# Hybrid decoder step on one core: where the first MLP's output is scaled for the time mixer, and when the residual is loaded

## The chip, the cores and the metric

The kernel runs on one core of a Trainium2 chip. Times are device microseconds of one execution, the median of three runs; the profile is of one further execution.

## The reference, cut to what matters

A decoder step of two layers: layer 0 mixes tokens with a Conformer convolution, layer 1 with RWKV-7 time mixing, and each is followed by a squared-ReLU MLP. The program has 1048 tokens (16 meta tokens, 1024 of the prompt, 8 decode tokens), a width of 1024 and a hidden width of 4096. What the change touches is the seam between the layers.

```python
def _rmsnorm(x, g):
    xf = x.astype(jnp.float32)
    y = xf * lax.rsqrt(jnp.mean(xf * xf, axis=-1, keepdims=True) + RMS_EPS)
    return (y * g.astype(jnp.float32)).astype(x.dtype)
...
def _rwkv7(h, shift_prev, S0, x_mix, ...):
    prev = jnp.concatenate([shift_prev[:, None, :].astype(h.dtype), h[:, :-1]], axis=1)
    xx = prev - h
    xr = h + xx * x_mix[0]      # and five more mixtures of h and xx
    ...
    out = ((yn + bonus).astype(h.dtype) * g) @ w_o
    return out, h[:, -1], S_final.astype(S0.dtype)
...
    for i in range(DEPTH):
        hn = _rmsnorm(h, norm_mix[i])
        ...                     # the mixer of this layer on hn
        h = h + out
        h = h + _sqrelu_mlp(_rmsnorm(h, norm_mlp[i]), w_mlp_in[i], w_mlp_out[i])
```

## The kernel before, in words

Activations lie with the width on the partitions: a tile of `[128, 8, n]` holds n tokens, the second index is the block of 128 channels (k-tile). The fp32 products are made of three fp32r matmuls of high and low parts: `split` (L159, L160) cuts a tile on ScalarE and VectorE or POOL, `load_w` (L165, L177, L182) loads and cuts weights, `mm3` (L211 to L213) multiplies.

The tokens are cut three ways. Layer 0 works on three groups G0 = (0, 352), (352, 348), (700, 348), as (first column, count). The RWKV mixer works on four groups G1 = (0, 272), (272, 256), (528, 256), (784, 264), called mixers 0 to 3 below. The mixer's output and the second MLP work on three groups G2 = (16, 328), (344, 352), (696, 352).

At the end of layer 0's MLP, `norm_out(g)` stores the residual h to `d_h` in DRAM, sums squares, makes the reciprocal root mean square `rs`, scales h in place by the norm's weights and `rs` (eight operations at L651, one for each k-tile) and stores the result to `d_hn`. `prepare(g)` of a mixer loads its columns of `d_hn` and the column before them into `hx` (L863, L865), makes the difference `xx` to the previous token (L869: six k-tiles on VectorE, two on POOL), and offers `mix(i, k)` (L892), which makes one k-tile of one of the six mixtures and splits it. `mixer_in(g)` makes the projections and the chunks' factors (names `rk`, `ab`, `wa`, `bv`), which go through DRAM; `advance` runs the recurrence over chunks of 64 tokens (`xa`, `sv`, `ni`), and its outputs go to `d_z`. `mixer_out(g)` loads the residual into h1 (L1633) and eight k-tiles of `d_z` into `zr` (L1639, three buffers), splits them, multiplies by `w_o` (tile `ps_oo`) and adds the products to h1 (L1643).

The stages overlap. The third group's first MLP with its `norm_out(2)` runs interleaved with mixer 0 (`beside_mixer`); what is left of it is finished before mixer 1 starts, where the pools of layer 0 are closed and those of the recurrence (`sv`, `xa`, set to zero on POOL) are opened in their place. `prepare(g+1)` runs inside the last phase of `mixer_in(g)`. `mixer_out(0)` runs while the recurrence goes on. Where instructions finally stand on each engine is decided when the program is built, by a scheduler that orders them by priorities and its own estimates; the tile framework inserts the waits.

Of the kernel before, what the change touches and what calls it, by code (L numbers as in the profile page):

```python
# [8 lines left out]
F32 = mybir.dt.float32  # L9
# [3 lines left out]
ALU = mybir.AluOpType  # L13
# [3 lines left out]
P = 128  # L17
D = 1024
KT = D // P
# [5 lines left out]
T = NP_TOK + DEC  # L25
# [5 lines left out]
G0 = [(0, 352), (352, 348), (700, 348)]  # L31
N0 = 352
G1 = [(0, 272), (272, 256), (528, 256), (784, 264)]
N1 = 272
# [14 lines left out]
def hybrid_step(tc, x_prompt, x_sample, state_conv, state_shift, state_wkv, meta_tokens,  # L49
# [8 lines left out]
    nc = tc.nc  # L58
    ctx = ExitStack()
    with ctx:  # L60
        def pool(stack, name, bufs, **kw):
            return stack.enter_context(tc.tile_pool(name=name, bufs=bufs, reuse_waits="tile", **kw))
# [10 lines left out]
        dram = pool(ctx, "dram", 1, space=bass.MemoryType.DRAM)  # L73
        d_x2 = dram.tile([P, KT, G0[2][1]], F32, name="d_x2")
        d_h = dram.tile([P, KT, T], F32, name="d_h")
        d_hn = dram.tile([P, KT, T], F32, name="d_hn")
        d_rk = dram.tile([P, KT, 2, T], F32, name="d_rk")
        d_ab = dram.tile([NCH, P, KT, 2, 2 * HS], F32, name="d_ab")
        d_v = dram.tile([NCH * HS, D], F32, name="d_v")
# [29 lines left out]
        for name, ap in vecs:  # L109
            n = ap.shape[0]  # L110
# [7 lines left out]
        def vec(name, i):  # L118
            c = col[name] + i
            return pvec[:, c:c + 1]  # L120

        cur = {}
# [34 lines left out]
        def split(hi, lo, src, eng_lo):  # L157

            nc.scalar.copy(hi, src)  # L159
            eng_lo.tensor_sub(lo, src, hi.bitcast(F32))  # L160
# [80 lines left out]
        def tt(name, tag):  # L241
            return cur["tmp"].tile([P, cur["n"]], F32, name=name, tag=tag)
# [19 lines left out]
        def mean_bcast(accs, n, name):  # L262

            ps = bank(f"st_{name}", "x")
            for i, acc in enumerate(accs):
                nc.tensor.matmul(ps[:, :n], ones_d, acc[:, :n], start=i == 0, stop=i == len(accs) - 1)
            return ps

        def square_sums(n, name, place, engs, tag="acc"):


            out, first = [], []

            def add(k, src):
                sq = place(k)
                nc.scalar.activation(sq, src, AF.Square)
                i = k % len(engs)
                if k >= KT - 2:
                    out.append(sq)
                elif k < len(engs):  # L280
                    first.append(sq)
                else:
                    if k < 2 * len(engs):
                        out.append(stat(f"acc_{name}{i}", f"{tag}{i}", 1))
                        a, b = out[i][:, :n], first[i]
                    else:
                        a = b = out[i][:, :n]
                    engs[i].tensor_add(a, b, sq)
            return add, out

        def rstd_of(ps, n, eps_i, name, tag="rs", bufs=2):
            sd = stat(f"sd_{name}", "sd", 1)
            nc.scalar.activation(sd[:, :n], ps[:, :n], AF.Sqrt, bias=eps_t[:, eps_i:eps_i + 1])
            rs = stat(f"rs_{name}", tag, bufs)
            nc.vector.reciprocal(rs[:, :n], sd[:, :n])
            return rs
# [117 lines left out]
        with ExitStack() as le:  # L414
# [221 lines left out]
            def norm_out(g):  # L636

                c0, n = G0[g]
                hv = h[g][:, :, :n]
                nc.sync.dma_start(d_h[:, :, c0:c0 + n], hv)  # L640
                if g < 2:
                    add, parts = square_sums(n, f"d{g}", lambda k: u[g][:, k, :n], (nc.gpsimd,), "accd")
                else:
                    add, parts = square_sums(n, f"d{g}", lambda k: tt(f"sqd{k}", "t1")[:, :n], (nc.gpsimd, nc.vector))
                for k in range(KT):
                    add(k, hv[:, k, :])
                    yield MW / KT
                rs = rstd_of(mean_bcast(parts, n, f"d{g}"), n, 0, f"d{g}", "rs" if g < 2 else "rsm")
                yield 1
                for k in range(KT):  # L650
                    nc.vector.scalar_tensor_tensor(hv[:, k, :], hv[:, k, :], vec("norm_mix", KT + k), rs[:, :n],  # L651
                                                   op0=ALU.mult, op1=ALU.mult)
                    yield 1
                nc.sync.dma_start(d_hn[:, :, c0:c0 + n], hv)
# [32 lines left out]
            with ExitStack() as s:  # L687
# [35 lines left out]
                for i, parts in enumerate((((1, rwkv_w1[0]), (4, rwkv_a1[0])), ((5, rwkv_g1[0]),))):  # L723
                    own, prev = (xin.tile([P, D], F32, name=f"lr{i}{s_}", tag="xt").rearrange("p (k c) -> p k c", k=KT) for s_ in "op")
                    w = P // len(parts)
# [128 lines left out]
        def prepare(g):  # L854

            c0, n = G1[g]
            npr = min(c0 + n, NP_TOK) - c0
            nm = lambda s, *a: f"{s}{g}" + "".join(f"_{x}" for x in a)

            hx = hnp.tile([P, KT, 1 + N1], F32, name=nm("hx"), tag="hx")  # L860
            if g == 0:
                nc.gpsimd.memset(hx[:, :, 0:1], 0.0)
                nc.sync.dma_start(hx[:, :, 1:1 + n], d_hn[:, :, :n])  # L863
            else:
                nc.sync.dma_start(hx[:, :, :1 + n], d_hn[:, :, c0 - 1:c0 + n])  # L865
            yield
            xx = hnp.tile([P, KT, N1], F32, name=nm("xx"), tag="xx")
            for k in range(KT):
                (nc.gpsimd if k % 3 == 2 else nc.vector).tensor_sub(xx[:, k, :npr], hx[:, k, 0:npr], hx[:, k, 1:1 + npr])  # L869
                yield  # L870
            if npr < n:
                sst = cur["raw"].tile([P, D], F32, name="sst", tag="raw")
                nc.scalar.dma_start(sst[:DEC, :], state_shift[0])
                pv = bank("pv", "x")
                for k in range(KT):
                    nc.tensor.transpose(pv[:, k * DEC:(k + 1) * DEC], sst[:DEC, k * P:(k + 1) * P], ident[:DEC, :DEC])
                sps = hnp.tile([P, KT, DEC], F32, name=nm("sps"), tag="sps")
                nc.scalar.copy(sps.rearrange("p k b -> p (k b)"), pv[:, :KT * DEC])
                nc.vector.tensor_sub(xx[:, :, npr:n], sps, hx[:, :, 1 + npr:1 + n])
                so = cur["raw"].tile([P, D], F32, name="so", tag="raw")  # L880
                for half in range(2):
                    pv = bank(f"pso{half}", "x")
                    for q in range(4):
                        nc.tensor.transpose(pv[:DEC + 1, q * P:(q + 1) * P], hx[:, half * 4 + q, npr:npr + DEC + 1], ident)
                    nc.scalar.copy(so[:DEC + 1, half * 512:(half + 1) * 512], pv[:DEC + 1, :])
                nc.scalar.dma_start(o_shift_prompt[0], so[0:1, :])
                nc.scalar.dma_start(o_shift_sample[0], so[1:DEC + 1, :])

            def mix(i, k):

                t = (cur["mx"] or cur["tmp"]).tile([P, cur["wm"]], F32, name=nm("mx", i, k), tag="t2")
                nc.vector.scalar_tensor_tensor(t[:, :n], xx[:, k, :n], vec("x_mix", i * KT + k), hx[:, k, 1:1 + n],  # L892
                                               op0=ALU.mult, op1=ALU.add)
                hi, lo = (r.tile([P, cur["wm"]], F32R, name=nm("m" + q, i, k), tag="m" + q) for q, r in zip("hl", cur["mix"]))
                split(hi[:, :n], lo[:, :n], t[:, :n], nc.gpsimd if k % 3 else nc.vector)
                return hi[:, :n], lo[:, :n]

            prep[g] = mix, hx, sps if npr < n else None
# [716 lines left out]
        with ExitStack() as l1:  # L1615
# [13 lines left out]
            def mixer_out(g, residp, actp, fill, add, order=range(KT), early=None):  # L1629
                ready = None  # L1630
                lo, n = G2[g]
                h1 = hl[g] = residp.tile([P, KT, cur["wide"]], F32, name=f"h1_{g}", tag="h")
                nc.sync.dma_start(h1[:, :, :n], d_h[:, :, lo:lo + n])  # L1633
                if early:
                    ready = early(h1)
                z = new_act(actp, f"z{g}", cur["wide"])
                for p in range(KT):
                    t = tt(f"zr{g}{p}", "t1")
                    nc.sync.dma_start(t[:, :n], d_z[:, p, lo:lo + n])  # L1639
                    split(z[0][:, p, :n], z[1][:, p, :n], t[:, :n], nc.vector)  # L1640
                for i, m in enumerate(order):
                    ps = dense(load_col(rwkv_w_o[0], m, f"wo{g}_{m}", nc.vector if early else nc.gpsimd), z, n, f"oo{g}_{m}", fill)
                    nc.vector.tensor_add(h1[:, m, :n], h1[:, m, :n], ps[:, :n])  # L1643
                    add(i, h1[:, m, :n])
                    if ready:
                        ready(m)
                    fill()
# [270 lines left out]
            n = G2[2][1]  # L1918
            ops, early, late = strassen_acts(g1, n, actp3, residp)
# [4 lines left out]
            rs = []  # L1924
# [49 lines left out]
```

## Time and profile before

| | us |
|---|---|
| runs | 2746.97, 2756.64, 2761.95; median 2756.64 |
| profiled execution | 2760.69, its span 2758.7 |
| TensorE busy | 2585.6 |
| VectorE busy | 2074.5 |
| POOL busy | 1710.2 |
| ScalarE busy | 1404.5 |

The span is the profiled stretch of the one execution; its time has 2 us more around it. Busy times overlap, and matmuls are pipelined, so a busy TensorE is not TensorE at its peak.

### The profile page before, as it was taken

The page shows a single profiled execution, that of the slowest core. Times are in us where ns is not written, and L with a number is a line of the kernel's source. Part 1 is how long each engine was busy: PE and PEld are TensorE (multiplying, and loading weights), DVE is VectorE, ACT ScalarE, POOL GpSimd, SP SyncE. Part 2 cuts the span into 40 slices and gives each one's busy share as a digit, 9 for nine tenths or more (in the row PEclk, how much of TensorE's full clock was granted, in tenths as well). Part 3 has the DMA queues.
Part 4 walks back from the last instruction along what each step waited for, and adds up shares of the span by engine and source line. Part 5 has one row for each costly group of instructions (what it writes and reads, how often), then busy time and mean ns, then how long its engine had stood idle before and what let it go on. Part 6 is the DMA issues. An engine that isn't in the chain of part 4 may idle for free.

```text
span 2758.7 us, 54194 instructions
## 1 busy us (share of the span) xinstructions
PE 2585.6 (94%) x20362; PEld 2495.6 (90%) x20362; DVE 2074.5 (75%) x3868; ACT 1404.5 (51%) x2614; POOL 1710.2 (62%) x2259
## 2 busy tenths in 40 slices
PE   8998999999998999997898798979989999999998
PEld 7998999899997999996788687768989998999998
DVE  5999999997456554677988887677897687566565
ACT  5545444553355444565675775655544564333333
POOL 6686877887787444554553544547648856556663
PEclk9998999999999999999999999989999999999999
DMA  6563544445445446668796886887657642222221
GB/s 181 159 192 92 161 132 137 134 148 164 138 131 150 146 142 179 185 199 220 204 241 187 219 221 175 198 230 186 178 140 232 175 131 78 76 70 77 69 77 58
DMA packets 659283, 428.30 MB, mean 155 GB/s; under 512 B 126840, under 2 KB 609208, under 8 KB 659022
## 3 DMA queue, kind: packets, MB, share of 16 engines
q1 hardware_dynamic: 652780, 421.93, 55.0%
q10 hardware_dynamic: 6018, 2.89, 0.4%
q8 instruction: 160, 2.62, 0.4%
q14 instruction: 101, 0.83, 0.1%
q0 software_dynamic: 224, 0.03, 0.0%
HBM read 353.03 MB, written 72.66 MB: 154 GB/s over the span
## 4 chain that ended last, share of the span: by engine, by line
PE 64%; DVE 15%; DMA 7%; POOL 5%; ACT 4%; issue 4%; SPq 0%; POOLq 0%; ACTq 0%; DVEq 0%
PE ps_in L212 4%; PE ps_in L213 4%; PE ps_in L211 4%; PE out L212 4%; PE out L213 4%; PE out L211 4%; PE os L213 3%; PE os L211 3%; PE os L212 3%; POOL wo_lo L182 2%; POOL wi_lo L182 2%; DVE cv L552 2%; PE su L211 1%; PE su L213 1%; PE su L212 1%
## 5 line engine op out<-in xcount | busy, mean ns | idle before, releaser
L182 POOL TENSOR_TENSOR wo_lo<-wo_raw,wo_hi 128x256 fp32r<-128x256 f32 x512 | 398.1, 810 | 188.1 <-ACT wo_hi L177 149.0
L182 POOL TENSOR_TENSOR wi_lo<-wi_raw,wi_hi 128x256 fp32r<-128x256 f32 x472 | 373.3, 824 | 161.0 <-ACT wi_hi L177 150.3
L552 DVE SCALAR_TENSOR_TENSOR cv<-u,wdw,cv 128x352 f32<-128x352 f32 (+2 forms) x720 | 376.4, 572 | 0.7
L211 PE MATMUL out<-hh,wo_hi 128*128 128x348 f32 (+2 forms) x1024 | 332.2, 328 | 17.8 <-DVE h L382 6.9
L212 PE MATMUL out<-hh,wo_lo 128*128 128x348 f32 (+2 forms) x1024 | 330.8, 324 | 2.6 <-DVE wo_lo L182 2.6
L211 PE MATMUL ps_in<-m_h,wi_hi 128*128 128x348 f32 (+2 forms) x1024 | 329.7, 322 | 2.2 <-ACT wi_hi L177 1.4
L212 PE MATMUL ps_in<-m_h,wi_lo 128*128 128x348 f32 (+2 forms) x1024 | 328.6, 321 | 2.4 <-POOL wi_lo L182 2.4
L213 PE MATMUL ps_in<-m_l,wi_hi 128*128 128x348 f32 (+2 forms) x1024 | 327.8, 321 | 0.0
L213 PE MATMUL out<-hl,wo_hi 128*128 128x348 f32 (+2 forms) x1024 | 327.1, 323 | 0.0
L382 DVE TENSOR_TENSOR h<-h,out 128x348 f32<-128x348 f32 (+2 forms) x512 | 249.8, 503 | 68.8 <-PE out L213 68.1
L177 ACT CAST wo_hi<-wo_raw 128x1024 fp32r<-128x1024 f32 x152 | 159.3, 1049 | 203.0 <-PE ps_in L213 104.9
L177 ACT CAST wi_hi<-wi_raw 128x1024 fp32r<-128x1024 f32 x128 | 134.2, 1049 | 235.0 <-PE out L213 105.2
L211 PEld LDWEIGHTS out<-hh,wo_hi 128*128 128x128 f32 x1024 | 194.0, 190 | 24.7 <-DVE h L382 8.2
L212 PEld LDWEIGHTS out<-hh,wo_lo 128*128 128x128 f32 x1024 | 195.1, 191 | 4.5 <-DVE wo_lo L182 3.2
L211 PEld LDWEIGHTS ps_in<-m_h,wi_hi 128*128 128x128 f32 x1024 | 192.8, 188 | 4.6 <-ACT wi_hi L177 2.6
L212 PEld LDWEIGHTS ps_in<-m_h,wi_lo 128*128 128x128 f32 x1024 | 192.6, 188 | 3.8 <-POOL wi_lo L182 2.8
L213 PEld LDWEIGHTS out<-hl,wo_hi 128*128 128x128 f32 x1024 | 193.5, 190 | 1.0 <-DVE hl L160 0.5
L213 PEld LDWEIGHTS ps_in<-m_l,wi_hi 128*128 128x128 f32 x1024 | 192.3, 188 | 0.8 <-DVE m_l L305 0.2
L1859 DVE TENSOR_TENSOR h<-h,os 128x352 f32<-128x352 f32 x256 | 126.5, 515 | 58.7 <-PE os L213 58.2
L212 PE MATMUL os<-hhs,wos_lo 128*128 128x352 f32 x512 | 165.1, 323 | 0.0
L213 PE MATMUL os<-hls,wos_hi 128*128 128x352 f32 x512 | 164.1, 323 | 0.0
L211 PE MATMUL os<-hhs,wos_hi 128*128 128x352 f32 x512 | 155.3, 323 | 0.1
(501 smaller groups left out, 8040.3 us busy)
## 6 DMA issues: line engine op xcount, KB each, us to landing
wi_raw<-in_w_mlp_in_dram SPq DMA_DIRECT2D x128, 512.0 KB
wo_raw<-in_w_mlp_out_dram SPq DMA_DIRECT2D x128, 512.0 KB
wk_raw<-in_rwkv_w_k_dram SPq DMA_DIRECT2D x32, 512.0 KB
wr_raw<-in_rwkv_w_r_dram SPq DMA_DIRECT2D x32, 512.0 KB
wv_raw<-in_rwkv_w_v_dram SPq DMA_DIRECT2D x32, 512.0 KB
d_ab<-ab SPq DMA_DIRECT2D x32, 512.0 KB
ws_raw<-in_w_mlp_in_dram SPq DMA_DIRECT2D x32, 512.0 KB
wos_raw<-in_w_mlp_out_dram SPq DMA_DIRECT2D x32, 512.0 KB
```

The costliest lines, as they stand in the source:

```text
L177: nc.scalar.copy(hi[:, :a * b], raw[:, :a * b])
L182: eng_lo.tensor_sub(lo[:, cs], raw[:, cs], hi[:, cs].bitcast(F32))
L211: nc.tensor.matmul(ps, w[0], act[0], start=first, stop=False, **kw)
L212: nc.tensor.matmul(ps, w[1], act[0], start=False, stop=False, **kw)
L213: nc.tensor.matmul(ps, w[0], act[1], start=False, stop=last, **kw)
L382: nc.vector.tensor_add(hv[:, 4 * i + m, :], hv[:, 4 * i + m, :], ps[:, :n])
L552: nc.vector.scalar_tensor_tensor(acc[m][:, :n], ug[:, m, j:j + n], wdw[:, m, j:j + 1], acc[m][:, :n], op0=ALU.mult, op1=ALU.add)
L1859: nc.vector.tensor_add(hv[:, 4 * i + m, :], hv[:, 4 * i + m, :], ps[:, :n])
```

## The change

Layer 0's third group is no longer scaled before it is stored: `norm_out(2)` stores only `rs`, 348 factors on each partition, to a new DRAM tensor `d_rs`, and `d_hn` ends at column 700. Mixers 2 and 3, whose columns lie wholly or partly past 700, load those from the unscaled `d_h`, load the factors (`rsx`), and scale in `hx` (eight operations each, of 84 and 265 columns). Mixer 0's `hx` is loaded in two halves of four k-tiles. In `mixer_out(0)` and `(1)` the residual is loaded in four pieces, behind the eight `zr` loads in the program; group 2 keeps its order.

```diff
-        d_hn = dram.tile([P, KT, T], F32, name="d_hn")
+        d_hn = dram.tile([P, KT, G0[2][0]], F32, name="d_hn")
+        d_rs = dram.tile([P, G0[2][1]], F32, name="d_rs")
...
                 rs = rstd_of(mean_bcast(parts, n, f"d{g}"), n, 0, f"d{g}", "rs" if g < 2 else "rsm")
                 yield 1
+                if g == 2:
+                    nc.sync.dma_start(d_rs, rs[:, :n])
+                    return
                 for k in range(KT):
                     nc.vector.scalar_tensor_tensor(hv[:, k, :], hv[:, k, :], vec("norm_mix", KT + k), rs[:, :n],
...
-                nc.sync.dma_start(hx[:, :, 1:1 + n], d_hn[:, :, :n])
+                for k in range(0, KT, 4):
+                    nc.sync.dma_start(hx[:, k:k + 4, 1:1 + n], d_hn[:, k:k + 4, :n])
             else:
-                nc.sync.dma_start(hx[:, :, :1 + n], d_hn[:, :, c0 - 1:c0 + n])
+                a, e, b = c0 - 1, c0 + n, G0[2][0]
+                if a < b:
+                    nc.sync.dma_start(hx[:, :, :min(b, e) - a], d_hn[:, :, a:min(b, e)])
+                if e > b:
+                    b = max(a, b)
+                    w, o = e - b, b - a
+                    rs = cur["tmp"].tile([P, N1], F32, name=nm("rsx"), tag="t2")
+                    nc.sync.dma_start(rs[:, :w], d_rs[:, b - G0[2][0]:e - G0[2][0]])
+                    nc.sync.dma_start(hx[:, :, o:o + w], d_h[:, :, b:e])
+                    for k in range(KT):
+                        hk = hx[:, k, o:o + w]
+                        nc.vector.scalar_tensor_tensor(hk, hk, vec("norm_mix", KT + k), rs[:, :w], op0=ALU.mult, op1=ALU.mult)
+                        if k % 4 == 3:
+                            yield
...
-                nc.sync.dma_start(h1[:, :, :n], d_h[:, :, lo:lo + n])
                 if early:
+                    nc.sync.dma_start(h1[:, :, :n], d_h[:, :, lo:lo + n])
                     ready = early(h1)
...
+                for m in range(0, 0 if early else KT, 2):
+                    nc.sync.dma_start(h1[:, m:m + 2, :n], d_h[:, m:m + 2, lo:lo + n])
```

Line numbers move by up to 18 in the changed program (L892 becomes L910, L1639 becomes L1657). At the end of `norm_out(2)` VectorE's instructions stood like this before:

```order
L1142 TENSOR_TENSOR bv_6_14313<-vv_6_14139,pk_6_14311 128x272
L1172 SCALAR_TENSOR_TENSOR rk_7_14050<-rk_7_14050,negs,pb_7_14315 128x272
L651 SCALAR_TENSOR_TENSOR h_2_9452<-h_2_9452,pvec,rs_d_14249 128x348 x8
L182 TENSOR_TENSOR wk_2_lo<-wk_2_raw,wk_2_hi 128x1024
L892 SCALAR_TENSOR_TENSOR mx_0_0_14963<-xx_12911,pvec,hx_12876 128x256
L892 SCALAR_TENSOR_TENSOR mx_0_1_14969<-xx_12911,pvec,hx_12876 128x256
L892 SCALAR_TENSOR_TENSOR mx_0_2_14975<-xx_12911,pvec,hx_12876 128x256
L1191 TENSOR_TENSOR wa_7_14213<-rk_7_14050,wa_7_14213 128x544
```

In the changed program the same place of VectorE reads:

```order
L1160 TENSOR_TENSOR bv_6_14312<-vv_6_14141,pk_6_14310 128x272
L1190 SCALAR_TENSOR_TENSOR rk_7_14052<-rk_7_14052,negs,pb_7_14314 128x272
L910 SCALAR_TENSOR_TENSOR mx_0_0_14957<-xx_12913,pvec,hx_12878 128x256
L183 TENSOR_TENSOR wk_2_lo<-wk_2_raw,wk_2_hi 128x1024
L910 SCALAR_TENSOR_TENSOR mx_0_1_14963<-xx_12913,pvec,hx_12878 128x256
L910 SCALAR_TENSOR_TENSOR mx_0_2_14969<-xx_12913,pvec,hx_12878 128x256
L1209 TENSOR_TENSOR wa_7_14215<-rk_7_14052,wa_7_14215 128x544
```

The eight scalings (x8 on one row) are gone, and the next weight split and the mixtures `mx` of mixer 1 move up behind `rk`. On SP's queue, at the start of `mixer_out(0)`, the residual stood ahead of the first three `zr` before (`bk`, `vt` and `ni` belong to the recurrence, `ez` to its outputs):

```order
L1241 DMA ni_22652<-d_n 128x1024
L1409 DMA d_y<-yt_22957 512x1x64 x2
L1633 DMA h_0_22594<-d_h 128x8x328
L1639 DMA zr_22598<-d_z 128x328
L1639 DMA zr_22602<-d_z 128x328
L1639 DMA zr_22606<-d_z 128x328
L1275 DMA bk_23054<-d_ab 64x8x128
L1277 DMA bk_23054<-d_ab 64x8x64
L1541 DMA d_z<-ez_0_22859 128x4x128
```

In the changed program SP's queue has there:

```order
L1259 DMA ni_22670<-d_n 128x1024
L1657 DMA zr_22612<-d_z 128x328
L1657 DMA zr_22616<-d_z 128x328
L1657 DMA zr_22620<-d_z 128x328
L1660 DMA h_0_22609<-d_h 128x2x328 x4
L1427 DMA d_y<-yt_22975 512x1x64 x2
L1559 DMA d_z<-ez_0_22877 128x4x128
L1293 DMA bk_23072<-d_ab 64x8x128
L1295 DMA bk_23072<-d_ab 64x8x64 x2
L1302 DMA vt_23080<-d_v 64x8x64
L1657 DMA zr_22624<-d_z 128x328
```

The three `zr` moved ahead of the residual's four pieces and of `d_y`, and the fourth `zr` stands behind the loads of the next chunk. In `prepare(3)` the eight scalings on VectorE of the changed program stand among the factors of mixer 2 (`wa`, `ab`, `rk`) and the recurrence's `xa`:

```order
L1209 TENSOR_TENSOR wa_0_18695<-rk_0_18626,wa_0_18695 128x2x256
L881 SCALAR_TENSOR_TENSOR hx_18664<-hx_18664,pvec,rsx_18665 128x265 x8
L1221 TENSOR_TENSOR ab_0_18725<-rk_0_18626,ex_0_18717 128x4x128
L1212 SCALAR_TENSOR_TENSOR rk_0_18723<-rk_0_18626,pvec,wa_0_18695 128x256
L1222 TENSOR_TENSOR ab_0_18725<-wa_0_18695,em_0_18715 128x4x128
L887 TENSOR_TENSOR xx_18838<-hx_18664 128x256
L1221 TENSOR_TENSOR ab_1_18904<-rk_1_18628,ex_1_18896 128x4x128
L887 TENSOR_TENSOR xx_18838<-hx_18664 128x256 x3
L1315 TENSOR_TENSOR xa_14458<-A_18432,m_ar 64x2x64
L1315 TENSOR_TENSOR xa_14458<-A_18440,m_ar 64x2x64
L887 TENSOR_TENSOR xx_18838<-hx_18664 128x256 x2
```

The scalings are new there; `xx`, which before stood ahead of the last `xa` and `nr` of a chunk, now stands behind them and around `ab_1`. On SP the factors `rsx` are loaded behind a weight load (`wv_5`) in this `prepare`.

## Rows read from the trace of the kernel before

**Rows 1.** Page: busy times of the engines, and the chain by engine.

```profile
PE 2585.6 (94%) x20362; PEld 2495.6 (90%) x20362; DVE 2074.5 (75%) x3868; ACT 1404.5 (51%) x2614; POOL 1710.2 (62%) x2259
...
PE 64%; DVE 15%; DMA 7%; POOL 5%; ACT 4%; issue 4%; SPq 0%; POOLq 0%; ACTq 0%; DVEq 0%
```

**Rows 2.** Windows, end of the third group's MLP; columns as in its first line.

```profile
core 0: us, PE busy (x) PEld busy (x) DVE busy (x) ACT busy (x) POOL busy (x), PEclk, DMA share, GB/s
1240.00:1260.00 20.00, 10.26 (x101) 8.58 (x99) 19.88 (x35) 14.59 (x35) 7.62 (x12) 0.96 0.61 173
1260.00:1280.00 20.00, 16.68 (x140) 15.33 (x141) 15.89 (x30) 11.10 (x24) 19.53 (x27) 0.79 1.02 232
```

**Rows 3.** Chain of waits, 1226 to 1345 us: start, duration, what.

```profile
1251.36 5.42 DVE h L651 x7
1265.90 5.15 DMA d_ab<-ab
```

**Rows 4.** Timeline of PE there: start, duration, instruction, [idle before <-releaser].

```profile
1260.01 1.22 PE L1040 MATMUL pn<-sq,hsel 128*128 128x256 f32 x2 [6.71 <-ACT sq L1050]
1264.11 0.65 PE L1122 MATMUL nn<-ab 64*32 64x32 f32 x32 [2.88 <-DVE ab L1204]
```

**Rows 5.** Timeline, 870 to 900 us: DVE and PE around mixer 0's load.

```profile
883.48 1.41 DVE L869 TENSOR_TENSOR xx<-hx 128x272 f32<-128x272 f32 x2 [5.77 <-DMA hx<-d_hn]
...
885.77 3.66 DVE L869 TENSOR_TENSOR xx<-hx 128x272 f32<-128x272 f32 x4
...
890.03 0.51 DVE L369 SCALAR_TENSOR_TENSOR r<-ps_in,rs_m 128x348 f32<-128x348 f32 x1
...
892.57 0.81 PE L211 MATMUL out<-hh,wo_hi 128*128 128x348 f32 x3 [4.08 <-ACT wo_hi L177]
```

**Rows 6.** Timeline, 1820 to 1860 us: the first mixer output.

```profile
1826.74 4.31 SPq L1639 DMA_DIRECT2D zr<-d_z  x3
...
1836.12 0.46 ACT L159 CAST z_h<-zr 128x328 fp32r<-128x328 f32 x1 [9.44 <-DMA zr<-d_z]
...
1836.64 0.64 PE L211 MATMUL ps_oo<-z_h,wo_hi 128*128 128x328 f32 x1 [10.74 <-ACT z_h L159]
...
1858.10 1.30 DVE L1643 TENSOR_TENSOR h<-h,ps_oo 128x328 f32<-128x328 f32 x3
```

**Rows 7.** Windows around the same wait, columns as in rows 2.

```profile
1826.00:1836.60 10.60, 0.00 (x0) 0.00 (x0) 5.06 (x18) 1.13 (x3) 1.08 (x3) 0.50 1.13 326
1836.60:1842.00 5.40, 5.36 (x20) 5.37 (x21) 4.72 (x13) 1.86 (x4) 0.00 (x0) 0.50 0.96 217
```

**Rows 8.** Timeline of DVE, 1271 us.

```profile
1271.51 1.84 DVE L892 SCALAR_TENSOR_TENSOR mx<-xx,pvec,hx 128x256 f32<-128x256 f32 x2 [3.52 <-POOL ml L160]
```

**Rows 9.** Chain of waits: transfers after 1285 us.

```profile
1293.15 4.24 DMA p<-d_p
...
1352.58 5.61 DMA hx<-d_hn
...
1538.17 7.24 DMA hx<-d_hn
...
1840.62 5.71 DMA zr<-d_z
```

**Rows 10.** Groups by line, tile `ps_oo`: PE's idle time before, times it happened.

```profile
  ACT z_h L159: 11.1, 2
```

**Rows 11.** VectorE's prices: timeline near 1300 us; groups by line (ns, min/median/max).

```profile
1299.80 0.25 DVE L1247 TENSOR_TENSOR ni<-ni,tt 128x84 f32<-128x84 f32 x1
...
L892 DVE SCALAR_TENSOR_TENSOR mx<-xx,pvec,hx x96: 443/491/1285, 892.5 to 1739.2; 128x256 f32<-128x256 f32 x48, 128x272 f32<-128x272 f32 x24, 128x264 f32<-128x264 f32 x24
```

**Rows 12.** Windows, mixers 2 and 3, columns as in rows 2.

```profile
1380.00:1840.00 460.00, 396.32 (x5140) 360.75 (x5139) 359.95 (x684) 306.09 (x719) 215.50 (x316) 0.93 0.82 213
```

**Rows 13.** Timeline: SP's issues behind mixer 3's `hx`; DVE's wait for it.

```profile
1539.02 3.52 SPq L165 DMA_DIRECT2D wv_raw<-in_rwkv_w_v_dram  x2
...
1545.43 1.93 DVE L869 TENSOR_TENSOR xx<-hx 128x256 f32<-128x256 f32 x3 [0.26 <-DMA hx<-d_hn]
```

## The prediction, made before the change was run

> **What bounds the kernel now.** The page comes first. TensorE is busy for 94% of the span, VectorE for 75%, and the chain that ended last runs 64% on TensorE and 15% on VectorE [rows 1]. A change that only moves loads and vector work therefore pays where TensorE stands still, and the question is where that is near the four edited places. The table of stretches (windows) shows it around the end of the third group's MLP: from 1240 to 1260 us VectorE works 19.88 of 20 us while TensorE works 10.26, and in the next 20 us the DMA engines are full, at a share of 1.02 [rows 2]. VectorE bounds the first stretch, the DMA engines the next.
>
> The chain of waits around 1250 us goes straight through VectorE: seven of the eight scalings of h, for 5.42 us [rows 3]. TensorE's timeline shows the price: it stands 6.71 us before 1260 and 2.88 us before 1264 [rows 4].
>
> Two other places are waits for loads. Near 883 us VectorE waits 5.77 us for `hx`. The MLP's `r` of line 369 stands behind the differences `xx` in VectorE's order and starts at 890.03, and TensorE then waits 4.08 us [rows 5]. In the first mixer output TensorE stands 10.74 us until 1836.64, since ScalarE waits 9.44 us for `zr`. On SP's queue the residual load (`h`, 128x8x328) stands just ahead of the three `zr` loads of 1826.74 [rows 6]. In that stretch the DMA engines move 326 GB/s at a share of 1.13, and TensorE's granted clock is 0.50 (1.2 GHz) then and for the next 5.4 us, until 1842 [rows 7].
>
> **The change part by part.**
>
> *Third group's output.* Eight scalings go, and a store of 1392 KB becomes one of 174 KB. As the order shows, what follows on VectorE is the mixer's own work. The chain loses 5.42 us. Bounds: at most 6.71 + 2.88 = 9.6 us, the whole of TensorE's two stands; at least about 2 us, because the waits behind it are mixed: VectorE itself later stands 3.52 us for a POOL split, and POOL reaches that split only after the memsets of `sv` and `xa` [rows 4, 8]. Until now those stand behind the `d_hn` store, whose buffer they take over; that store is gone, so I expect no new wait there. The store's bytes are worth (1392 - 174) KB = 1.25 MB at 232 GB/s [rows 2] = 5.4 us of a full DMA stretch, but that lies beside the gain on VectorE and is not added. I take -5.4.
>
> *First mixer's `hx` in two halves.* The first half can let three of VectorE's six `xx` run while the second is under way. Six took 1.41 + 3.66 = 5.07 us [rows 5], so `r` comes about 2.5 us sooner; a small VectorE or ScalarE wait stays between, so I take -2.0. Bounds: -4.1, TensorE's wait, and 0, if halves are slower: a 512 KB transfer (`d_ab`) took 5.15 us in the full stretch while an `hx` of 8x257 columns (1.05 MB) took 5.61 [rows 3, 9], so half the bytes are not half the time.
>
> The Trainium skill, page "DMA: Bandwidth & Descriptors", section Bandwidth, asks for transfers of at least 1 MiB for 75% of peak, which speaks against this split and against the residual in four pieces. The two rows just named lean its way, though in different stretches. By it this term would be 0 and the sum 2.0 us worse; by the row of the six `xx` it is -2.0.
>
> *Residual behind `zr`.* The load is 128 x 8 x 328 x 4 B = 1.34 MB; at 326 GB/s that is 4.1 us in front of `zr`. Behind them it is still early: the first addition into `h` follows only after the first product, over 20 us later [rows 6]. I take -4.1. Bounds: 0, since only three `zr` fit in their buffers and the second three, at 1840.62, which took 5.71 us to land [rows 9], may still set the pace; -9.4, if the whole of ScalarE's wait goes. In the other two outputs this reordering can give nothing: of the 11.1 us that TensorE waited for `z` in all three, 10.74 were this one wait [rows 6, 10].
>
> *What is added.* Eight scalings of 128x84 in mixer 2. A VectorE operation of that shape took 0.25 us, so 2.0 us. Eight of 128x265 in mixer 3: the same kind of instruction at 128x256 to 272 took 0.49 us (median of 96), so 3.9 us [rows 11]. From 1380 to 1840 VectorE is busy 360 of 460 us, a share of 0.78, and TensorE 396 [rows 12]. No engine is full, so part of the 5.9 us falls into idle time: bounds 0 and +5.9; weighted with VectorE's share, +4.6, rounded up to +4.7 since the chains there pass through `xx`. The extra loads (174 KB of factors, a second `hx` piece) replace bytes that `d_hn` carried. In mixer 3 the order has the eight scalings in front of `ab_0`, `ab_1` and the masks `xa` of the recurrence, so what waits there waits on all of these.
>
> Sum: -5.4 - 2.0 - 4.1 + 4.7 = -6.8 us. The profiled execution took 2760.69 us, which gives 2753.9. It lay 4.05 us above the median of the runs, 2756.64, so on the scale of that median the forecast is **2750 us**. 0.5% (13.8 us) is about what a measurement of this kernel can tell from no change, so "faster" means below 2742.9 and "slower" above 2770.4.
>
> **The rivals.**
>
> *No gain (0.16).* TensorE is the bound for most of the span, and mixers 1 to 3 follow on the same recurrence; a start 5 us earlier meets full DMA engines (1.02 [rows 2]) or the next late load. For it: the load of `p` costs 4.24 us on the chain, whenever it starts [rows 9]. Against it: no load on that chain has a fixed hour, each starts when what it reads is there. The gains of 11.5 shrink to about the added 5.9 and the time stays near 2757.
>
> *More (0.20).* All three waits go at their upper bounds, -9.6 - 4.1 - 9.4 = -23.1, and the scalings cost +3 to +4.7: about -20, so 2737 us. For it: after its stand TensorE runs 20 matmuls in 5.4 us at 1.2 GHz [rows 7], and what that costs would go with the stand. Against it: three engines would have to be ready at once.
>
> *Slower: the scaling waits for late loads (0.14).* VectorE takes its instructions in order, so the scalings hold up `ab` and what else stands behind them until both `hx` pieces and the factors are there. In mixer 3 the factors are issued behind a 512 KB weight load, whose two issues took 3.52 us on SP [rows 13]. On the chain the `hx` loads stood 5.61 and 7.24 us [rows 9]. If both waits appear again in full on VectorE: -11.5 + 5.9 + 12.85 = +7.3, so about 2764 us. It decides from waits of 5.6 us together. Against it: VectorE's wait for mixer 3's load was 0.26 us [rows 13], since it is issued well ahead of its use.
>
> The same page, section Specifications, puts full rate at rows of 512 bytes or more; the new 84-column load has rows of 336 bytes. No run yet shows such a row; the nearest, `p` with rows of 128 bytes, landed in 4.24 us, no later than the long ones. If its 344 KB cost twice, an estimate of 3.7 us from 5.61 us for 1.05 MB, mixer 2's wait alone would not reach the deciding point.
>
> **How the numbers follow.** The forecast has 0.50; its own range, with the first term between -2 and -9.6 and the added work between 0 and +5.9, is 2743 to 2757. No gain 0.16, more 0.20, slower 0.14. The range 2736 to 2763 holds the forecast, no gain, most of "more" and half of "slower"; the bounds of all terms together would be 2756.64 - 23.1 = 2733.5 and 2756.64 + 12.9 + 5.9 - 11.5 = 2764. Faster by over 0.5%: "more" and a small part of the forecast, 0.25. Slower by over 0.5%: only where the late-load case is worse than worked out or the scheduler's new order brings a wait I did not see, 0.08. Within 0.5%: 0.67.
>
> **What would show it.** Right: no scaling of h near 1251, and TensorE's stand before 1260 falls from 6.71 to about 2; the first `zr` lands about 5 us after its issue, and the stand of 10.74 falls to about 6.5; VectorE's wait for `hx` near 880 falls by about 3 us; the new scalings of mixers 2 and 3 start after waits under 1 us. Wrong: those scalings wait several us for `rsx` or `hx`; TensorE stands as long as before at 1260 behind a POOL or DMA step; or the second three `zr` become the wait in the mixer's output.

## The result, and the profile after

The changed kernel takes 2790.18 us (median of 6 runs, 2785.22 to 2797.50), the kernel before 2755.21 us in the same comparison (6 runs). The ratio is 1.0129, with a 95% interval of 1.0107 to 1.0151: slower by 1.3%, where 2750 us, and at most 2763, were forecast.

The page of the changed kernel, which answers to [rows 1], its busy times:

```profile
span 2790.4 us, 54217 instructions
PE 2613.1 (94%) x20362; PEld 2514.0 (90%) x20362; DVE 2074.3 (74%) x3876; ACT 1403.4 (50%) x2614; POOL 1713.0 (61%) x2259
```

The same 20362 matmuls keep TensorE busy for 27.5 us longer (2613.1 against 2585.6), and the span grew by 31.7. VectorE's time is unchanged. So most of the loss is no new wait: TensorE spends more time on the same work. To find where, the ends of stages on TensorE are compared by their last matmul (the times come from the timelines; the last column is an experiment told below, the changed kernel with one burst moved):

| end of | before | after | burst moved |
|---|---|---|---|
| mixer 1, `p_r` | 1347.7 | 1348.3 | 1346.4 |
| mixer 1, `p_v` | 1415.1 | 1438.1 | 1426.4 |
| mixer 2, `p_r` | 1528.4 | 1541.7 | 1527.0 |
| mixer 2, `p_v` | 1612.8 | 1633.4 | 1615.4 |
| mixer 3, `p_v` | 1806.8 | 1828.2 | 1807.0 |
| first mixer output, products | 1880.7 | 1898.8 | 1874.3 |
| span | 2758.7 | 2790.4 | 2761.0 |

Up to the end of mixer 1's `p_r` no loss shows. One execution differs from another by some us here: in three kernels told below, which change the mixer output alone, this mark stands at 1339.8, 1342.1 and 1344.5. In the next phase, where `p_v` is multiplied and the steps of `prepare(2)` stand, 23 us go. The windows of the kernel before there, with the columns of [rows 2]:

```profile
1400.00:1410.00 10.00, 10.00 (x136) 8.97 (x123) 7.80 (x17) 5.72 (x16) 0.11 (x2) 1.00 1.00 292
1410.00:1420.00 10.00, 9.19 (x166) 8.14 (x166) 9.91 (x24) 9.50 (x28) 3.30 (x7) 1.00 0.77 206
1420.00:1430.00 10.00, 7.71 (x121) 6.59 (x118) 9.94 (x13) 8.80 (x20) 8.65 (x8) 1.00 0.96 245
```

And of the changed kernel:

```profile
1400.00:1410.00 10.00, 9.98 (x138) 8.02 (x140) 9.39 (x22) 6.13 (x18) 2.69 (x5) 1.00 0.92 251
1410.00:1420.00 10.00, 10.00 (x66) 6.68 (x60) 1.31 (x2) 4.70 (x11) 2.11 (x2) 0.97 0.74 168
1420.00:1430.00 10.00, 10.00 (x74) 7.57 (x74) 2.96 (x6) 3.56 (x8) 0.00 (x0) 0.52 0.23 54
```

TensorE is busy for all of both later windows, but with 66 and 74 matmuls instead of 166 and 121, and the other engines run out of work. In the second its granted clock falls to about half (1.2 GHz) although it never stood still. TensorE's timeline of the changed kernel shows what it does (start, duration, instruction):

```profile
1410.28 0.38 PE L212 MATMUL p_v<-mh,wv_hi 128*128 128x256 f32 x1
1410.60 0.33 PE L1383 MATMUL Y<-uv,nr 128*64 128x64 f32 x2
1410.85 0.39 PE L213 MATMUL p_v<-mh,wv_lo 128*128 128x256 f32 x1
1411.18 0.33 PE L1383 MATMUL Y<-uv,nr 128*64 128x64 f32 x2
...
1420.42 0.58 PE L212 MATMUL p_v<-mh,wv_hi 128*128 128x256 f32 x1
1420.94 0.31 PE L1335 MATMUL gg<-x,no 32*32 32x32 f32 x2
1421.18 0.58 PE L213 MATMUL p_v<-mh,wv_lo 128*128 128x256 f32 x1
...
1430.12 0.28 PE L212 MATMUL p_v<-mh,wv_hi 128*128 128x256 f32 x1
1430.24 0.28 PE L213 MATMUL p_v<-mh,wv_lo 128*128 128x256 f32 x1
```

The scheduler has dealt the products `Y` and `gg` of the recurrence's chunk 1 singly between those of `p_v`: one product on a 128*128 tile, one on small tiles (an fp32 product, which the trace counts as x2), one on a 128*128 tile, and so on. From one `p_v` to the next 0.57 us pass with `Y` between them, 0.49 with `gg`, and 0.75 with `gg` at the lower clock; where `p_v` stands behind `p_v` (1430.12, 1430.24), 0.12. Before, the small ones stood together, on TensorE's timeline of that kernel:

```profile
1419.23 1.10 PE L1365 MATMUL Y<-uv,nr 128*64 128x64 f32 x32
1420.26 0.69 PE L1317 MATMUL gg<-x,no 32*32 32x32 f32 x32
```

From 1410.28 to 1424.95 the changed kernel runs 24 `p_v`, 20 `Y` and 32 `gg` in 14.67 us. At the grouped prices that is 24 x 0.12 + 20 x 1.03 / 32 + 0.69 = 4.2 us. Two shorter passages (l_w and l_a with `Y` at 1406, `p_v` with `po` at 1433) cost 2.2 us more than grouped, each, by the same reckoning: together some 15 of the 23 us. About 4 of the rest are chunk 1's `S`, `Y` and `gg`, which before came after the end of `p_v`; some 2 are the work behind the passage, at half clock until 1429. By the end of mixer 2's `p_r` 13 of the 23 us are left: from `p_r` to `p_r` the kernel before takes 180.7 us, the changed one 193.4, and with the burst moved it is 180.6.

The Trainium skill, page "TensorEngine Tiling (Array Packing)", section Tiling Modes, says that a change of the tiling mode, unlike a change of the tile alone, drains TensorE. This trace fits that without proving it: a turn with `Y` takes 0.57 us where 0.12 + 2 x 0.034 = 0.19 were due, 0.38 more. But with the tile's shape the number format changes too, since `p_v` is made of fp32r products and `Y` and `gg` are fp32. TensorE's timeline of the kernel before shows a change of format alone, all on 128*128 tiles (`A` is fp32, `p_k` fp32r):

```profile
1288.30 0.59 PE L1290 MATMUL A<-xa,bk 128*128 128x256 f32 x2
1288.55 0.47 PE L212 MATMUL p_k<-mh,wk_lo 128*128 128x256 f32 x1
1288.85 0.28 PE L213 MATMUL p_k<-ml,wk_hi 128*128 128x256 f32 x1
1288.97 0.28 PE L211 MATMUL p_k<-mh,wk_hi 128*128 128x256 f32 x1
```

Behind `A` a `p_k` takes 0.30 us until the next starts, behind `p_k` 0.12: the format alone can cost 0.18 a turn. How the 0.38 divides between shape and format, no run tells; "the passage" below means the alternation of both.

### The profile page after: what moved, and what is told of

Same layout as the page of the kernel before. It is cut to its first block, busy times and chain, and to the rows that moved or that the text cites. A ratio compares the mean times of both kernels' runs of the same rounds, so it can differ in the third digit from the quotient of the medians.

```text
span 2790.4 us, 54217 instructions
## 1 busy us (share of the span) xinstructions
PE 2613.1 (94%) x20362; PEld 2514.0 (90%) x20362; DVE 2074.3 (74%) x3876; ACT 1403.4 (50%) x2614; POOL 1713.0 (61%) x2259
```

## The experiments

**Which parts it takes.** Theory 1: the loss is a matter of the order that the scheduler builds, and so comes and goes with combinations of parts. Theory 2: the scalings and their loads cost it. Theory 3: the mixer output does. Four kernels hold some of the parts. Without the mixer output's part:

```diff
+                nc.sync.dma_start(h1[:, :, :n], d_h[:, :, lo:lo + n])
                 if early:
-                    nc.sync.dma_start(h1[:, :, :n], d_h[:, :, lo:lo + n])
...
-                for m in range(0, 0 if early else KT, 2):
-                    nc.sync.dma_start(h1[:, m:m + 2, :n], d_h[:, m:m + 2, lo:lo + n])
```

> The change without its part in the mixer output (residual loaded first again). In this build's order TensorE still alternates 70 times in one run between the projection p_v (128x128 tiles) and the recurrence's Y and gg (64x64 and 32x32), as in the full change. Theory 1 (the alternation costs, about 0.2 us each time the tile shape changes, some 16 us in two blocks of p_v, and the rest follows from it): about 2790 us, 2783 to 2797. Theory 2 (the scalings and the late loads in mixers 2 and 3 hold up VectorE): also about 2790. Theory 3 (the residual's place in the mixer output): about 2755 or less.

Without the halves:

```diff
-                for k in range(0, KT, 4):
-                    nc.sync.dma_start(hx[:, k:k + 4, 1:1 + n], d_hn[:, k:k + 4, :n])
+                nc.sync.dma_start(hx[:, :, 1:1 + n], d_hn[:, :, :n])
```

> The change without the two halves of the first mixer's hx. Unscaled third group, scalings in mixers 2 and 3, and the residual behind zr are all there; but in this build's order the long alternation of p_v with Y and gg is absent (changes of tile shape on TensorE 259 in the whole program, 270 before, 341 with the full change). Theory 1: 2740 to 2757, the gains forecast without the run of alternations. Theory 2: still 2780 or more, since every scaling and late load is in it. Theory 3: 2780 or more.

The kernel before with the mixer output's part alone:

> The kernel before with only the residual behind zr in the mixer output. Theory 1: 2745 to 2756, a gain of 0 to 9 us (4.1 by the prediction). Theory 3: 2780 or more.

The kernel before with the halves alone:

> The kernel before with only the first mixer's hx in two halves. The order has no long alternation (268 changes of tile shape). Theory 1: 2748 to 2757 (2 us less than before by the prediction). Theory 4 (the split load itself is slow, wherever it stands): 2775 or more.

Measured, against 2756.24 us of the kernel before in the same comparison; a passage here is a stretch of TensorE's timeline in which a single 128*128 product stands between smaller tiles again and again:

| kernel | us | ratio (95%) | passage in mixer 1 |
|---|---|---|---|
| third group + halves | 2776.03 | 1.0071 (1.0056 to 1.0086) | 38 turns, 1402 to 1433 |
| third group + mixer output | 2763.33 | 1.0028 (1.0016 to 1.0039) | none |
| mixer output alone | 2769.26 | 1.0048 (1.0031 to 1.0064) | none |
| halves alone | 2752.65 | 0.9984 (0.9971 to 0.9996) | none |

The full change has the same 38 turns in mixer 1. Of these builds only those with both the third group's part and the halves have them. Only the expectation for the halves alone came true: by theory 1 the first kernel should have been 7 us slower than it was, the second 6 and the third 13 us faster, and theories 2 and 3 miss the first two by more. The mixer output's part loses by itself, where -4.1 us was forecast.

**Another number of pieces.** If the order and not the halves as such makes the passage, four pieces may escape it. The changed kernel, and the one without the mixer output's part, each with

```diff
-                for k in range(0, KT, 4):
-                    nc.sync.dma_start(hx[:, k:k + 4, 1:1 + n], d_hn[:, k:k + 4, :n])
+                for k in range(0, KT, 2):
+                    nc.sync.dma_start(hx[:, k:k + 2, 1:1 + n], d_hn[:, k:k + 2, :n])
```

> The full change with the first mixer's hx loaded in four quarters in place of two halves, nothing else. The two extra loads shift the scheduler's order: the run of 70 changes of tile shape between p_v and the recurrence is gone (269 changes in the program, 341 with halves). Theory 1 (that alternation is what the change costs in mixer 1, about 20 us, and the residual's place 7 to 13 us): 2760 to 2770. Theory 2 (scalings and late loads of mixers 2 and 3): 2785 to 2795, since they are unchanged.

> As the run before, and the residual loaded ahead of zr as in the kernel before. Theory 1: 2746 to 2756, the gains forecast for the third group's output less the scalings. If the scalings cost what theory 2 says: 2775 or more. If only the residual's place is wrong in the full change: 2755 or less here and above 2765 in the run before.

Measured against 2756.05 us: 2761.97, ratio 1.0023 (1.0012 to 1.0034), and 2757.95, ratio 1.0007 (0.9997 to 1.0016). Neither has a passage in mixer 1. The first lies where theory 1 had it, the second 2 us above. Two more transfers thus make the change 28 us faster than it is with halves, which no cost of a transfer explains.

**The burst moved.** The next test touches neither loads nor vector work: only the priority of chunk 1's products `S`, `Y` and `gg`, so that they no longer fall between those of `p_v`. In the changed kernel, and in the one without the mixer output's part:

```diff
-        def burst(lead, rest):
+        def burst(lead, rest, off=None):
...
-            with tc.high_priority(offset=BURST):
+            with tc.high_priority(offset=off or BURST):
...
-            burst(ss[:2], rest)
+            burst(ss[:2], rest, 500 if c == 1 else None)
```

> The full change with one number changed for one burst: the products of the recurrence's chunk 1 (S, Y and the next gg) get a priority offset of 500 in place of 400. The orders of TensorE agree up to the place of the long alternation; there the burst now stands in one piece (268 changes of tile shape in place of 341), behind it rows move a little. Theory 1: the full change less about 20 us, 2763 to 2775. Theory 2 (scalings and late loads) and any theory by which only the number of loads or their sizes count: 2785 to 2795.

> The same without the change's part in the mixer output. Theory 1: the 2776 us of that build less about 20 us, 2750 to 2762. Theory 2: 2776 as before.

Measured against 2754.73 us: 2763.24, ratio 1.0027 (1.0016 to 1.0039), and 2757.87, ratio 1.0015 (1.0005 to 1.0026): 27 and 18 us faster than the same kernels with the passage, as theory 1 forecast. TensorE's timeline of the first now has `Y` and `gg` together ahead of `p_v`, and `p_v` behind `p_v`:

```profile
1402.99 1.13 PE L1383 MATMUL Y<-uv,nr 128*64 128x64 f32 x32
1404.05 0.69 PE L1335 MATMUL gg<-x,no 32*32 32x32 f32 x32
...
1409.07 0.28 PE L212 MATMUL p_v<-mh,wv_hi 128*128 128x256 f32 x1
1409.18 0.28 PE L213 MATMUL p_v<-mh,wv_lo 128*128 128x256 f32 x1
...
1420.53 0.58 PE L214 MATMUL p_v<-ml,wv_hi 128*128 128x256 f32 x1
1421.04 0.31 PE L1335 MATMUL po<-p,gg 32*32 32x32 f32 x2
1421.28 0.58 PE L212 MATMUL p_v<-mh,wv_hi 128*128 128x256 f32 x1
```

A short passage with `po` stays at 1420. By the table of stages, of the 29.4 us between the two spans 12.8 lie between mixer 1's `p_r` and mixer 2's `p_r`, where the passage stood; 14.7 come later, in many places, since the order behind it is another too, and no single place is shown for them.

**More room for every burst.** If the passage is the trouble, a larger offset for all bursts might help as well. The kernel before, and the one without the mixer output's part, with

```diff
-        BURST = 400
+        BURST = 600
```

> The kernel before with one number of its scheduling changed: the bursts of the recurrence get a priority offset of 600 in place of 400, so the scheduler breaks into them less (249 changes of tile shape on TensorE, 270 before). Theory 1: 2740 to 2757. If the number of changes were no guide to the time: anything from 2740 to 2780.

> The change without its part in the mixer output, with the two halves of hx, and the same priority offset of 600: 256 changes of tile shape, no run of more than 20. Without that offset the same edits took 2776 us. Theory 1: 2742 to 2760. Theory 2 (scalings and late loads): 2776 as before.

Measured against 2752.10 us: 2769.35, ratio 1.0060 (1.0037 to 1.0082), and 2783.57, ratio 1.0112 (1.0088 to 1.0136). Both forecasts of theory 1 missed. No passage stands in mixer 1, and still the two take 199.6 and 204.3 us from mixer 1's `p_r` to mixer 2's, longer than the changed kernel. In the new order TensorE waits for a load and for VectorE instead; its longest waits in the second, 1390 to 1460 us (engine, tile, line, releaser: us in all, times, longest):

```profile
PE A L1308 <- DMA bk<-d_ab: 4.5, 1, 4.5
PE p_k L213 <- DVE wk_lo L183: 3.3, 1, 3.3
PE p_v L212 <- DVE n L1144: 2.4, 1, 2.4
```

So few turns are no sign of a fast kernel; the order can lose in more ways than one.

**Without the scalings.** The kernel with quarters and without the mixer output's part, without `rsx` and the sixteen scalings in `prepare`:

```diff
-                    rs = cur["tmp"].tile([P, N1], F32, name=nm("rsx"), tag="t2")
-                    nc.sync.dma_start(rs[:, :w], d_rs[:, b - G0[2][0]:e - G0[2][0]])
...
-                    for k in range(KT):
-                        hk = hx[:, k, o:o + w]
-                        nc.vector.scalar_tensor_tensor(hk, hk, vec("norm_mix", KT + k), rs[:, :w], op0=ALU.mult, op1=ALU.mult)
```

> The change without its part in the mixer output, with hx in quarters, and without what it adds: the factors are not loaded and the scalings of mixers 2 and 3 are left out, so these mixers work on unscaled columns. With them the time was 2758 us, 280 changes of tile shape here and 277 there. If the scalings cost what the prediction took: 4 to 6 us less, 2752 to 2754. If they are hidden: 2756 to 2760. If the third group's output alone gains what was forecast and they take it back: 2750 or less.

Measured against 2754.73 us: 2768.89, ratio 1.0062 (1.0044 to 1.0081). Less work made it slower: with the scalings the same kernel stood at 1.0007. Every expectation missed. From `p_r` to `p_r` it takes 196.7 us, again without the passage of 38 turns. A price of some us can't be measured in this kernel by taking work out, since the order made anew moves the time by more.

**The mixer output, by group.** The kernel before, with the residual behind `zr` only in `mixer_out(0)`, and only in `mixer_out(1)`; the first:

```diff
-                nc.sync.dma_start(h1[:, :, :n], d_h[:, :, lo:lo + n])
+                if g:
+                    nc.sync.dma_start(h1[:, :, :n], d_h[:, :, lo:lo + n])
...
+                for m in range(0, 0 if g else KT, 2):
+                    nc.sync.dma_start(h1[:, m:m + 2, :n], d_h[:, m:m + 2, lo:lo + n])
```

> The kernel before with the residual behind zr in mixer_out(0) alone. Theory 5 (the first output's products, started 8 us earlier, push the recurrence's next chunk back on TensorE and VectorE): most of the 13 us of the run with both groups, 2762 to 2769. Theory 6 (the second output's four late pieces): 2752 to 2757 here.

> The kernel before with the residual behind zr in mixer_out(1) alone. Theory 5: 2752 to 2759, no change. Theory 6: 2762 to 2769.

Measured against 2756.05 us: 2765.52, ratio 1.0034 (1.0022 to 1.0046), and 2755.86, ratio 1.0005 (0.9994 to 1.0015). The loss is group 0's; group 1 shows none. TensorE's timeline of the kernel with group 0's part at the place of [rows 6], and two later waits:

```profile
1799.20 0.46 PE L1122 MATMUL nn<-ab 64*32 64x32 f32 x32 [3.08 <-DVE ab L1204]
...
1821.01 0.64 PE L211 MATMUL ps_oo<-z_h,wo_hi 128*128 128x328 f32 x1 [2.36 <-ACT z_h L159]
...
1832.73 0.42 PE L211 MATMUL ps_oo<-z_h,wo_hi 128*128 128x328 f32 x1 [2.43 <-ACT z_h L159]
...
1867.91 0.63 PE L211 MATMUL ps_in<-m_h,wi_hi 128*128 128x328 f32 x1 [4.15 <-ACT m_h L304]
...
1871.75 0.64 PE L213 MATMUL ps_in<-m_l,wi_hi 128*128 128x328 f32 x1 [2.93 <-DVE m_l L305]
```

The stand of 10.74 us became 2.36 and 2.43: the mechanism works, by 5.95 us. Some of it is given back ahead of it, where VectorE now stands 3.69 us for `ey` (timeline, 1797.37; 0.37 before) in front of the `ab` that TensorE waits for, and behind it, where the MLP's first products wait 4.15 and 2.93 us for the sums in `h`. These waits show where the gain goes, not all of the 9.5 us between the medians: this one execution's span is 2760.4 us, only 1.7 above that of the kernel before.

**The alternation by itself.** Behind the end of the kernel before stands a block of 96 turns, each one fp32r product of 256 columns on a 128*128 tile and two fp32 ones of 64 columns on 128*64 tiles (four in the trace), that nothing else competes with; and the same products, wide ones first and then the narrow ones:

```diff
+            seq = [x for i in range(N) for x in ((wide, i), (half_, 0), (half_, 1))]
...
-            seq = [x for i in range(N) for x in ((wide, i), (half_, 0), (half_, 1))]
+            seq = [(wide, i) for i in range(N)] + [(half_, i) for i in range(2 * N)]
```

> The kernel before with a block of matmuls added behind its end, which computes nothing of the output: 96 times one matmul of 128x128 weights on 256 columns (fp32r) and two of 64 columns into the two halves of a 64-column tile (fp32), in turns. Theory 1: each turn takes clearly longer than its two kinds do by themselves; from the rows of the changed kernel (one p_v and two Y in 0.57 us at the full clock) 0.45 to 0.65 us a turn, 43 to 62 us for the block. Rival (the matmuls themselves were slow there, for another reason): as long as in the grouped block of the next run.

> The same 96 and 192 matmuls in two groups, first all of one kind, then all of the other. Theory 1: 0.11 us for each of the 96 and 0.04 to 0.11 us for each of the 192, together 18 to 32 us. Rival: the same time as in turns.

One run each: 2843.78 and 2773.78 us, beside 2752.10 of the kernel before. A window ahead of the alternating block and one inside it, columns as in [rows 2]:

```profile
2746.00:2751.50 5.50, 0.57 (x3) 0.14 (x1) 0.47 (x3) 0.68 (x1) 0.00 (x0) 0.50 0.50 167
2770.00:2790.00 20.00, 20.00 (x110) 12.57 (x106) 0.00 (x0) 0.00 (x0) 0.00 (x0) 0.50 0.00 1
```

And inside the grouped block, with TensorE's timeline of it:

```profile
2750.00:2755.00 5.00, 5.00 (x44) 5.00 (x43) 0.00 (x0) 0.00 (x0) 0.00 (x0) 1.00 0.00 0
...
2746.18 13.09 PE L1952 MATMUL altb<-alta,altw 128*128 128x256 f32 x96 [5.02 <-DVE alta L1950]
2759.20 11.42 PE L1953 MATMUL alts<-ident 128*64 128x64 f32 x384
```

The last of the alternating products ended some 89 us after the first: 0.93 us a turn, against (13.09 + 11.42) / 96 = 0.255 grouped. The alternating block took longer than the 43 to 62 us expected, the grouped one lies inside its 18 to 32. The clock stood at 0.50 when either block began; it rose in the grouped one and stayed in the other. By an estimate from these rows that explains at most a factor of 2, 0.51 us; the other 0.4 us is the alternation's, of shape and format together. In the kernel, at full clock and with one small product a turn in place of two, a turn costs 0.57.

## Why the prediction was wrong

**The step that failed** is the sum. It has a term for each edited place and none for the order of the rest. Of that the prediction says only that a loss would come where "the scheduler's new order brings a wait I did not see", inside a chance of 0.08. What came was for the most part no wait: 27.5 of the 31.7 us of span are busy time of TensorE. The order of TensorE's products in mixer 1's `p_v` phase, which the prediction read at no place, alternates between tile shapes and number formats. Moving one burst's priority takes back 27 of the 35 us. About 13 us of that are lost and won where the passage stands; the rest comes from the order behind it, and for that part the runs name no single place. The forecast's own range doesn't follow from its terms either: they give 2741 to 2754, not 2743 to 2757, and the measured time lies far above both.

**Third group's output (-5.4).** The mechanism is as forecast. TensorE's timeline of the changed kernel, for [rows 4]:

```profile
1256.04 0.70 PE L1058 MATMUL pn<-sq,hsel 128*128 128x256 f32 x2 [2.21 <-ACT sq L1068]
1258.62 0.45 PE L1140 MATMUL nn<-ab 64*32 64x32 f32 x32 [1.88 <-DVE ab L1222]
...
1306.50 0.58 PE L212 MATMUL p_g<-hxh,g_hi 128*128 128x256 f32 x1 [5.63 <-ACT g_hi L178]
```

The stands shrank from 6.71 to 2.21 and from 2.88 to 1.88, together by 5.5 us. But at 1306.50 TensorE waits 5.63 us for a weight cast, and mixer 1's `p_r` ends at 1348.3 against 1347.7, so no gain shows there. The rival "no gain", by the next late step, is what happened here; the prediction gave it to the whole, not to this term.

**`hx` in halves (-2.0).** Right in kind, somewhat small: alone it gave 2752.65 against 2756.24, -3.6 us, inside its bounds, though the order behind it is another too. VectorE's and TensorE's timelines of the changed kernel, for [rows 5]:

```profile
881.37 0.44 DVE L887 TENSOR_TENSOR xx<-hx 128x272 f32<-128x272 f32 x1 [4.67 <-DMA hx<-d_hn]
...
893.74 0.75 PE L212 MATMUL out<-hh,wo_hi 128*128 128x348 f32 x3 [1.29 <-ACT wo_hi L178]
```

VectorE's wait fell by 1.1 us, not by 3, but TensorE's by 2.8. The rule of 1 MiB from the Trainium skill's page "DMA: Bandwidth & Descriptors", section Bandwidth, would have made this term 0; here the kernel with two loads of about half a MiB each was 3.6 us faster.

**Residual behind `zr` (-4.1).** The sign is wrong: +9.5 us for group 0 alone, 0 for group 1. The wait fell by more than forecast, in the changed kernel from 10.74 to 5.51 us; the bounds stopped at 0 because they held only the waits at the moved loads. Nothing in the step says what stands behind them. In the changed kernel VectorE's timeline shows the last sums of `h` dealt among the steps `tt` and `ni` of an inverse, and TensorE's shows the wait for `z_h` and the one that those sums cost:

```profile
1900.42 0.48 DVE L1663 TENSOR_TENSOR h<-h,ps_oo 128x328 f32<-128x328 f32 x1
1900.83 0.44 DVE L1265 TENSOR_TENSOR ni<-ni,tt 128x168 f32<-128x168 f32 x1
...
1905.86 0.49 DVE L1663 TENSOR_TENSOR h<-h,ps_oo 128x328 f32<-128x328 f32 x1
...
1910.05 0.49 DVE L1663 TENSOR_TENSOR h<-h,ps_oo 128x328 f32<-128x328 f32 x1
```

```profile
1857.16 0.64 PE L212 MATMUL ps_oo<-z_h,wo_hi 128*128 128x328 f32 x1 [5.51 <-ACT z_h L160]
...
1910.48 0.64 PE L212 MATMUL ps_in<-m_h,wi_hi 128*128 128x328 f32 x1 [10.34 <-ACT m_h L305]
```

The products ended at 1898.8, the last sum at 1910.5; before, the two were 3.5 us apart (1880.7 and 1884.2). By the table of stages 18.1 us of the loss stand when these products end and 13.6 arise behind them; with the burst moved 8.7 still do.

**The scalings (+4.7).** The rival that they wait for late loads is refuted, but the second eight were longer than forecast. VectorE's timeline of the changed kernel, with no wait ahead of either eight:

```profile
1373.47 2.28 DVE L881 SCALAR_TENSOR_TENSOR hx<-hx,pvec,rsx 128x84 f32<-128x84 f32 x8
...
1564.03 5.63 DVE L881 SCALAR_TENSOR_TENSOR hx<-hx,pvec,rsx 128x265 f32<-128x265 f32 x8
```

2.28 us stand against 2.0 forecast and 5.63 against 3.9, together 7.9 against 5.9, and VectorE never stood idle ahead of any of the sixteen. What they cost the span stays open, as told above.

**The parts together.** With the passage out of the way (quarters, or the burst moved) the change still loses 6 to 9 us, and without the mixer output's part 2 to 3. The best of all runs is the halves alone, 0.9984 (0.9971 to 0.9996).

## What to carry to other kernels

In a kernel whose order a scheduler makes, a local edit's price is the edit plus a new order of everything behind it: here a changed priority alone moved the time by 8 to 27 us, more than any term of the sum. So compare the bounding engine's whole order before and after, and look for long runs in which its tile shapes and number formats alternate and for steps of one chain dealt among another's. A busy engine is no proof of work done: count its instructions in a window.

## What the runs showed of the hardware

TensorE, dealt fp32r products on 128*128 tiles and fp32 products on 128*64 tiles in turn, needed 0.93 us a turn where the same products grouped took 0.255. The granted clock was 0.50 ahead of both blocks; it stayed there for the whole 89 us of turns, though TensorE showed 100% busy, and rose to 1.00 in the grouped block. In the changed kernel the clock fell from 1.00 to 0.50 at about 1419.5 us, while TensorE ran such turns without an idle moment. At one tile shape, 128*128, the first fp32r product behind an fp32 one took 0.30 us until the next started, where 0.12 passed between fp32r products of that size.
